# More gathered tokens in the expert layer: 112 instead of 96, one-hots weighed on ScalarE, gate matrices loaded in five parts

## The chip, the cores and the metric

One Trainium2 chip, of which the program uses one core. The metric is the device time of one execution in microseconds (us); less is better. The kernel before took 2694.28 us, the median of three runs between 2692.90 and 2695.57. The engines are TensorE (PE; PEld is its weight load), VectorE (DVE), ScalarE (ACT), GpSimd (POOL) and SyncE (SP). Each also issues DMAs, in the order of its own instructions.

## The reference

Two blocks on 512 tokens of 1024 channels, in float32. The first mixes (pooling, a state-space layer) and then runs the expert layer of this case. The second (linear attention, S5, a feed-forward network) isn't touched. Its weights and intermediate results are float32, and each has to be met closely.

```
q  = (h @ w_query)                      # 8 heads, two halves of 128
s1, s2 = scores of the halves against 128 + 128 sub-keys
v1, i1 = top_k(s1, 16);  v2, i2 = top_k(s2, 16)
top_s, pos = top_k(all 256 sums v1 + v2, 16)
idx   = i1[...] * 128 + i2[...]         # one of 16384 experts
gates = softmax(top_s)                  # 8 heads x 16 experts for each token
act   = gelu(h . expert_down[idx])      # one number per token and expert
out   = sum over (gates * act) * expert_up[idx]
```

So each token uses 128 of 16384 experts.

## The kernel before, in words

The expert layer treats its tokens in two ways. The first TG = 96 tokens are *gathered*: for each group of tokens in `GROUPS` an indirect DMA (`fetch`, L756) fetches one expert row of 1024 numbers into each of the 128 partitions, tile `row`, in 3 buffers; `dot` (L764) multiplies it with the token (VectorE, sum into `dots`). Later `weigh` (L767) takes Gelu of the dots and multiplies by the gates, and `add` (L784) fetches the row of the other matrix and adds it, weighed, to `tsum` on VectorE. A group of n tokens takes n fetches for the dots and n for the adds. The other TD = 416 tokens are *dense*: all 16384 experts are computed for them, in 128 tiles of 128 experts, and a gate matrix that is zero nearly everywhere picks out those that count.

*Down pass*, tile j: the weights are loaded (`load_w`: `raw` by SyncE's DMA, split by ScalarE into `hi`, L118, and by VectorE into the remainder `lo`, L119), then 24 matmuls (`mm3`, L126 to L128: hi x hi, hi x lo, lo x hi for 8 blocks of 128 rows) with 416 columns give `ps`; ScalarE takes Gelu (L830) and every second tile is written to HBM, `act_d`.

*Up pass*, tile j: `aj` is read back from `act_d` (L1076), `gt` holds the gates of 8 tiles (L1068, read from `g_d`, two buffers), VectorE multiplies them into `wg` (L1084), ScalarE and VectorE split this into `wh` (L131) and `wl` (L132), and 24 matmuls of 416 columns add to eight accumulators. At the end a fold (L1104) adds the gathered tokens' sums.

Beside the down pass runs a list of small jobs, `fill`, each with a cost in microseconds; after each tile `run_fill` issues as many as a due time allows. It holds the choice of experts (`select`: top 16, softmax, and `ids`, L663 to L678), the turning of the result to token order, and `scatter` (L721 to L747): for 8 dense tokens at a time VectorE compares ids with a ramp (L734, one-hots `oh`), multiplies the one half by the exponent factor of the gates (L737, `gexp`) and the other by their mantissas (L740), PE multiplies both halves into gate matrices (L745), ScalarE copies them to `gst` (L746), and every 32 tokens a DMA of POOL's queue writes a chunk of `g_d` (13 chunks). Then come the dots and the first 48 adds. Beside the up pass the list holds the other 48 adds, the tables of the S5 layer (ending with two DMAs of 2112 KB, L1015 and L1016) and some of the conditioning.

The order on each engine is not that of the source alone. A scheduler reorders by a simulated time line; `soon()` gives the chain of weights and gates priority, and `issue_after` ties an instruction behind another. The gates of tiles 8J to 8J+7 are tied behind `hi` of tile 8(J-1), four DMAs in one go.

Of the kernel before, what the change touches and what calls it, by code (L numbers as in the profile page):

```python
# [59 lines left out]
def tile_blocks(ctx, tc, I, out):  # L60
# [500 lines left out]
    with tc.tile_pool(name="peert", bufs=2, reuse_waits="tile") as pt, tc.tile_pool(name="peer", bufs=1, reuse_waits="tile") as pe:  # L561
# [63 lines left out]
        gexp = pe.tile([P, TD], BF16, name="rows_ge")  # L625
# [3 lines left out]
        def select(t):  # L629
# [31 lines left out]
            sel = [pt.tile([P, 8, 16], F32, tag=f"sel{s}", name=nm("sel"), bufs=1) for s in range(2)]  # L661

            def ids(s):  # L663
# [3 lines left out]
                else:  # L667
                    nc.vector.tensor_scalar(pi, pos, 15, None, ALU.bitwise_and)
                pf = pt.tile([P, 8, 16], F32, tag="pf", name=nm("pf"), bufs=1)
# [38 lines left out]
            def gathered():  # L708
                fid = pt.tile([P, P], F32, tag="pf", name="fid", bufs=1)
# [14 lines left out]
        def scatter(t0):  # L724

            ch, off = divmod(t0, TC)
            if off == 0:
                gst[ch] = px.tile([P, P, TC], F32, tag="g", name=nm("gst"))
# [12 lines left out]
            for c in range(n):
                ps = psum()
                for i in range(4):
                    for a in range(2):
                        nc.tensor.matmul(ps[:, i * P : i * P + P], o1[:, c, :, i], o2[a][:, c, :, i], start=a == 0, stop=a == 1)  # L745
                nc.scalar.copy(  # L746
                    gst[ch][:, :, off + 4 * c : off + 4 * c + 4].rearrange("p j t -> p t j"), ps.rearrange("p (t j) -> p t j", j=P))  # L747
            if off + SC == TC:
# [98 lines left out]
    def s5_prepare(sp):  # L847
# [183 lines left out]
        fill.append((0.1, table_out))  # L1031

    with tc.tile_pool(name="s5p", bufs=1, reuse_waits="tile") as s5p, tc.tile_pool(name="up", bufs=2, reuse_waits="tile") as pu:
# [6 lines left out]
        def beside():  # L1040
# [715 lines left out]
```

## Time and profile before

| | us |
|---|---|
| median of 3 runs | 2694.28 |
| profiled execution, its own time | 2692.56 |
| its span | 2690.7 |
| PE busy | 2597.9 (97%) |
| VectorE busy | 1874.7 (70%) |
| ScalarE busy | 1070.4 (40%) |
| GpSimd busy | 473.8 (18%) |
| down pass | 428.40 to 1102.40 |
| up pass | 1110.30 to 1729.30 |

The profile is that of one execution. Busy time says what each engine did over the whole span; the work of a pass is read in its own stretch. The chain of waits follows the end of the program back, step by step, to what released it. A releaser in brackets (`<-`) is the engine and tile that an idle engine waited for. Matmuls overlap, so a matmul's own duration is longer than the time from one start to the next. The row of a DMA issue gives its size and the time to its landing. The granted clock of TensorE was 0.985 of full speed over the span.

### The profile page before, as it was taken

The page shows a single profiled execution, that of the slowest core. Times are in us where ns is not written, and L with a number is a line of the kernel's source. Part 1 is how long each engine was busy: PE and PEld are TensorE (multiplying, and loading weights), DVE is VectorE, ACT ScalarE, POOL GpSimd, SP SyncE. Part 2 cuts the span into 40 slices and gives each one's busy share as a digit, 9 for nine tenths or more (in the row PEclk, how much of TensorE's full clock was granted, in tenths as well). Part 3 has the DMA queues.
Part 4 walks back from the last instruction along what each step waited for, and adds up shares of the span by engine and source line. Part 5 has one row for each costly group of instructions (what it writes and reads, how often), then busy time and mean ns, then how long its engine had stood idle before and what let it go on. Part 6 is the DMA issues. An engine that isn't in the chain of part 4 may idle for free.

```text
span 2690.7 us, 36274 instructions
## 1 busy us (share of the span) xinstructions
PE 2597.9 (97%) x13752; PEld 2343.2 (87%) x13752; DVE 1874.7 (70%) x3438; ACT 1070.4 (40%) x1511; POOL 473.8 (18%) x495
## 2 busy tenths in 40 slices
PE   6999999999999999899999899899999999999997
PEld 5776789999999999898999899888998888688886
DVE  5777699998898888586789457666567644552543
ACT  4574333434534445334343233445432343432221
POOL 0001000343234333111121101100053300010100
PEclk9999999999999999999999899999999999999999
DMA  6224433789888889988897978322276554233331
GB/s 259 95 84 136 145 106 121 275 287 339 299 291 307 312 302 314 318 260 297 277 302 241 290 244 271 104 79 71 83 215 190 180 176 126 73 99 94 95 101 63
DMA packets 179374, 532.93 MB, mean 198 GB/s; under 512 B 20608, under 2 KB 55648, under 8 KB 177280
## 3 DMA queue, kind: packets, MB, share of 16 engines
q1 hardware_dynamic: 85040, 280.83, 31.6%
q0 software_dynamic: 42000, 159.80, 17.7%
q10 hardware_dynamic: 52160, 89.99, 9.8%
q8 instruction: 108, 1.77, 0.3%
q14 instruction: 66, 0.54, 0.1%
HBM read 448.98 MB, written 80.41 MB: 197 GB/s over the span
## 4 chain that ended last, share of the span: by engine, by line
PE 88%; DMA 4%; DVE 3%; issue 2%; ACT 1%; ACTq 1%; POOL 0%; SPq 0%; DVEq 0%; POOLq 0%
PE ps L127 26%; PE ps L126 26%; PE ps L128 26%; PE ps L745 4%; DMA gt<-g_d 2%; DMA mats_d<-bd 1%; ACTq L1068 1%; DVE lo L119 1%; PE ps L615 1%; PE ps L1443 1%; PE ps L148 0%; ACT hi L118 0%; DMA wa<-in_wada_dram 0%; PE ps L487 0%; DMA res<-in_x_t_dram 0%
## 5 line engine op out<-in xcount | busy, mean ns | idle before, releaser
L118 ACT ACTIVATE hi<-raw 128x1024 fp32r<-128x1024 f32 (+2 forms) x459 | 481.6, 1051 | 1131.4 <-PE ps L127 811.5
L119 DVE TENSOR_TENSOR lo<-raw,hi 128x1024 fp32r<-128x1024 f32 (+2 forms) x459 | 579.7, 1265 | 373.3 <-ACT hi L118 358.7
L126 PE MATMUL ps<-h2h,hi 128*128 128x416 f32 (+1 forms) x1152 | 412.3, 359 | 4.0 <-ACT h2h L569 3.0
L127 PE MATMUL ps<-h2l,hi 128*128 128x416 f32 (+1 forms) x1152 | 413.1, 359 | 2.9 <-DVE h2l L570 2.9
L128 PE MATMUL ps<-h2h,lo 128*128 128x416 f32 (+1 forms) x1152 | 412.5, 359 | 0.0
L127 PE MATMUL ps<-wl,hi 128*128 128x416 f32 x1024 | 364.2, 356 | 17.9 <-DVE wl L132 17.9
L126 PE MATMUL ps<-wh,hi 128*128 128x416 f32 x1024 | 356.5, 355 | 10.8 <-ACT wh L131 10.8
L128 PE MATMUL ps<-wh,lo 128*128 128x416 f32 x1024 | 363.1, 356 | 1.0 <-DVE lo L119 1.0
L126 PE MATMUL ps<-Ah,hi 128*128 128x512 f32 (+2 forms) x944 | 336.4, 360 | 6.7 <-ACT Ah L1592 3.7
L127 PE MATMUL ps<-Al,hi 128*128 128x512 f32 (+2 forms) x944 | 339.7, 360 | 2.7 <-DVE Al L1130 2.7
L128 PE MATMUL ps<-Ah,lo 128*128 128x512 f32 (+2 forms) x944 | 337.0, 357 | 0.0
L126 PEld LDWEIGHTS ps<-h2h,hi 128*128 128x128 f32 x1152 | 217.9, 189 | 11.6 <-ACT h2h L569 3.8
L127 PEld LDWEIGHTS ps<-h2l,hi 128*128 128x128 f32 x1152 | 217.8, 189 | 9.9 <-DVE h2l L570 3.6
L128 PEld LDWEIGHTS ps<-h2h,lo 128*128 128x128 f32 x1152 | 218.0, 189 | 6.5 <-DVE lo L119 0.4
L756 POOL DMA_INDIRECT row<-in_eu_dram,gid x96 | 129.9, 1353 | 518.8 <-DVE tsum L784 437.1
L127 PEld LDWEIGHTS ps<-wl,hi 128*128 128x128 f32 x1024 | 194.8, 190 | 23.8 <-DVE wl L132 20.2
L126 PEld LDWEIGHTS ps<-wh,hi 128*128 128x128 f32 x1024 | 195.9, 192 | 13.9 <-ACT wh L131 11.9
L126 PEld LDWEIGHTS ps<-Ah,hi 128*128 128x128 f32 x944 | 177.8, 189 | 33.1 <-ACT Ah L1592 4.5
L127 PEld LDWEIGHTS ps<-Al,hi 128*128 128x128 f32 x944 | 178.9, 189 | 29.7 <-DVE Al L1130 2.9
L128 PEld LDWEIGHTS ps<-Ah,lo 128*128 128x128 f32 x944 | 178.6, 189 | 25.5 <-issue 1.9
L128 PEld LDWEIGHTS ps<-wh,lo 128*128 128x128 f32 x1024 | 195.5, 191 | 2.6 <-DVE lo L119 1.4
L756 POOL DMA_INDIRECT row<-in_ed_r_dram,gid x96 | 147.5, 1537 | 256.5 <-DVE dots L764 139.8
(610 smaller groups left out, 4206.6 us busy)
## 6 DMA issues: line engine op xcount, KB each, us to landing
raw<-in_ed_dram SPq DMA_DIRECT2D x128, 512.0 KB, 5.2
raw<-in_eu_dram SPq DMA_DIRECT2D x128, 512.0 KB, 4.8
raw<-in_win_dram SPq DMA_DIRECT2D x67, 512.0 KB, 3.5
raw<-in_wff_dram SPq DMA_DIRECT2D x64, 512.0 KB, 3.8
g_d<-gst POOLq DMA_DIRECT2D x13, 2048.0 KB, 9.8
aj<-act_d ACTq DMA_DIRECT2D x63, 416.0 KB, 4.5
wa<-in_wada_dram SPq DMA_DIRECT2D x46, 512.0 KB, 4.6
gt<-g_d ACTq DMA_DIRECT2D x45, 512.0 KB, 9.1
```

The costliest lines, as they stand in the source:

```text
L118: top[0] = nc.scalar.activation(hi[:, :n], raw[:, :n], AF.Copy)
L119: low[0] = nc.vector.tensor_sub(lo[:, :n], raw[:, :n], hi[:, :n].bitcast(F32))
L126: nc.tensor.matmul(ps, wh, x[0], start=first, stop=False)
L127: nc.tensor.matmul(ps, wh, x[1], start=False, stop=False)
L128: nc.tensor.matmul(ps, wl, x[0], start=False, stop=last)
L615: nc.tensor.matmul(ps[:, t * P : t * P + P], q[:, t * P : t * P + P], skt[:, m], start=True, stop=True)
L745: nc.tensor.matmul(ps[:, i * P : i * P + P], o1[:, c, :, i], o2[a][:, c, :, i], start=a == 0, stop=a == 1)
L756: nc.gpsimd.indirect_dma_start(out=raw, out_offset=None, in_=src.rearrange("a b d -> (a b) d"), in_offset=bass.IndirectOffsetOnAxis(ap=gid ...
L1068: nc.scalar.dma_start(gt[:, c:c1, a:b], g_d[c:c1, :, j // 8 * 8 + a : j // 8 * 8 + b].rearrange("c p j t -> p c j t"))
L1443: nc.tensor.matmul(ps[:, 16 * i : 16 * i + 16], wk[:, i, j * P : j * P + P], wk[:, i, c0 : c0 + 16], start=j == 0, stop=j == 1)
```

## The change

- `GROUPS` gets a third group of 16 tokens: 112 gathered, 400 dense. All dense matmuls have 400 columns.
- The chunks of `g_d` hold 24 tokens, and the last 16 have a tensor of their own, `ge_d`: 16 chunks and one small.
- `scatter` multiplies the one-hots by the exponents on ScalarE, one instruction of 128x128 for each token (L745 of the changed kernel).
- In `ids` the positions are 16-bit numbers, and the sum over 16 places is made by halving.
- A dot is computed two fetches after its own (`dots_of`), `row` has 4 buffers. 96 dots and 56 adds are listed in the down pass; 16 dots, the weighing of groups two and three and 56 adds in the up pass. The due times and some buffers change with it.
- The gates of the next 8 tiles come in five DMAs (L1099 and L1101), each tied behind `hi` of another of the five tiles 8(J-1) to 8(J-1)+4. `wg` is made by two multiplies, of 384 and 16 columns (L1137 and L1138).
- The two 2112 KB DMAs of the S5 tables are issued in eight parts.

```diff
-    TC = 32
-    GROUPS = ((0, 64, 2), (64, 32, 4))
+    TC = 24
+    GROUPS = ((0, 64, 2), (64, 32, 4), (96, 16, 8))
     TG = sum(n for _, n, _ in GROUPS)
     TD = T - TG
-    NCH = TD // TC
+    NCH, TE = divmod(TD, TC)
     g_d = dp.tile([NCH, P, P, TC], F32, name="g_d")
+    ge_d = dp.tile([P, P, TE], F32, name="ge_d")
...
-                pf = pt.tile([P, 8, 16], F32, tag="pf", name=nm("pf"), bufs=1)
+                pf = pt.tile([P, 8, 16], F16, tag="pf", name=nm("pf"), bufs=1)
...
-                nc.vector.tensor_reduce(sel[s], eq, AX.X, ALU.add)
+                for n in (8, 4, 2):
+                    nc.vector.tensor_tensor(eq[:, :, :, :n], eq[:, :, :, :n], eq[:, :, :, n : 2 * n], ALU.add)
+                nc.vector.tensor_tensor(sel[s], eq[:, :, :, 0], eq[:, :, :, 1], ALU.add)
...
-            nc.vector.tensor_tensor(
-                o1, eq[:, :, 0], bc(gexp[:, t0 : t0 + SC].rearrange("p (c t) -> p c t", t=4).unsqueeze(2), [P, n, P, 4]), ALU.mult)
+            for t in range(SC):
+                nc.scalar.mul(o1[:, t // 4, :, t % 4], eq[:, t // 4, 0, :, t % 4], gexp[:, t0 + t : t0 + t + 1])
...
-            raw = gx.tile([P, D], F32, tag="row", name=nm("row"), bufs=3)
+            raw = gx.tile([P, D], F32, tag="row", name=nm("row"), bufs=4)
...
+        def dots_of(lag):
+            while len(asked) > lag:
+                g, i, raw = asked.pop(0)
...
         def dot(g, i):
-            raw = fetch(I["ed_r"], g, i)
...
+            asked.append((g, i, fetch(I["ed_r"], g, i)))
+            dots_of(2)
...
-        NOW, LAST = 48, 16
+        NOW, LAST = 56, 24
...
-        dots_, adds_ = [dot_of(p) for p in picks[n0:]], adds[: NOW - LAST]
+        dots_, adds_, left = [dot_of(p) for p in picks[n0 : n0 + 32]], adds[: NOW - LAST], [dot_of(p) for p in picks[n0 + 32 :]]
...
-        per = sum(c for c, _ in fill) / (P - 6)
+        per = sum(c for c, _ in fill) / (P - 10)
...
-            run_fill(min((j + 1) * per - done[0], 4.8))
+            run_fill(min((j + 1) * per - done[0], 5.0))
...
-        def table_out():
-            nc.gpsimd.dma_start(mats_d[:, :, MW - 2 * NC5 : MW - NC5], et["r"])
-            nc.gpsimd.dma_start(mats_d[:, :, MW - NC5 :], et["i"])
+        def table_out(a):
+            nc.gpsimd.dma_start(mats_d[:, a : a + 8, MW - 2 * NC5 : MW - NC5], et["r"][:, a : a + 8])
+            nc.gpsimd.dma_start(mats_d[:, a : a + 8, MW - NC5 :], et["i"][:, a : a + 8])
...
+        def gate_piece(to, b, i, j0, j1):
+            of = slice(8 * b + j0, 8 * b + j1)
+            if i < NPC - 1:
+                c = slice(4 * i, min(4 * i + 4, NCH))
+                nc.scalar.dma_start(to[0][:, c, j0:j1], g_d[c, :, of].rearrange("c p j t -> p c j t"))
+            else:
+                nc.scalar.dma_start(to[1][:, j0:j1], ge_d[:, of])
...
-                with tc.issue_after(tops[max(j - 8, 0)].ins) if j else ExitStack():
-                    for c in range(0, NCH, 4):
-                        c1 = min(c + 4, NCH)
-                        nc.scalar.dma_start(gt[:, c:c1, a:b], g_d[c:c1, :, j // 8 * 8 + a : j // 8 * 8 + b].rearrange("c p j t -> p c j t"))
...
+            with tc.issue_after(top[0].ins):
+                if j == 2:
+                    for i in range(NPC):
+                        gate_piece(cur, 0, i, 4, 8)
+                if j % 8 == 0 and j < P - 8:
+                    nxt = gate_tile()
+                if j % 8 < 5 and j < P - 8:
+                    for i in range(j % 8, NPC, 5):
+                        gate_piece(nxt, j // 8 + 1, i, 0, 8)
...
-                nc.vector.tensor_tensor(
-                    wg.rearrange("p (c t) -> p c t", t=TC), aj[j % 2].rearrange("p (c t) -> p c t", t=TC), gt[:, :, j % 8], ALU.mult)
+                nc.vector.tensor_tensor(v(wg), v(aj[j % 2]), gt[:, :, j % 8], ALU.mult)
+                nc.vector.tensor_tensor(wg[:, NCH * TC :], aj[j % 2][:, NCH * TC :], ge[:, j % 8], ALU.mult)
```

The change moves instructions; two places are shown. The first is the seam between the passes, on ScalarE. Before, with the gates of tiles 0 to 3 (`gt_1483`) and of tiles 8 to 15 (`gt_1540`) issued around the last but one Gelu (`at_`), and `hi` of tile 1 behind them (`hi_1493`):

```order
725 L1068 DMA gt_1483_10124<-g_d_2335 128x4x128 x3
726 L830 ACTIVATE at__1479_10067<-ps355_10036 128x416
727 L1068 DMA gt_1483_10124<-g_d_2335 128x128
728 L1068 DMA gt_1540_10506<-g_d_2335 128x4x256 x3
729 L1068 DMA gt_1540_10506<-g_d_2335 128x256
730 L118 ACTIVATE hi_1493_10170<-raw_1492_10169 128x1024
731 L830 ACTIVATE at__1479_10067<-ps356_10069 128x416
732 L118 ACTIVATE hi_1500_10212<-raw_1499_10211 128x1024
733 L832 DMA act_d_2336<-at__1479_10067 128x832
734 L1076 DMA aj_1498_10209<-act_d_2336 128x832
735 L131 ACTIVATE wh_1490_10140<-wg_1489_10139 128x416
```

Afterwards, from `wh` of tiles 0 and 1 (`wh_1493`, `wh_1499`) to `wh` of tile 2 (`wh_1506`); `gt_1485` are the gates of tiles 0 to 7, of which these are 4 to 7, and `gt_1491` those of tiles 8 to 15:

```order
789 L118 ACTIVATE hi_1503_10591<-raw_1502_10590 128x1024
790 L1099 DMA gt_1485_10501<-g_d_2335 128x4x96 x4
791 L1101 DMA gt_1485_10501<-ge_d_2336 128x64
792 L1099 DMA gt_1491_10517<-g_d_2335 128x4x192
793 L118 ACTIVATE hi_1509_10634<-raw_1508_10633 128x1024
794 L1099 DMA gt_1491_10517<-g_d_2335 128x4x192
795 L865 DMA s5in_10671<-in_s5_dram 128x2144
796 L205 DMA cs_1514_10685<-in_c_dram 128x1024
797 L118 ACTIVATE hi_1517_10691<-raw_1516_10690 128x1024
798 L1101 DMA gt_1491_10517<-ge_d_2336 128x128
799 L1117 DMA aj_1515_10688<-act_d_2337 128x800
800 L131 ACTIVATE wh_1506_10603<-wg_1505_10602 128x400
```

What moved: the gate transfers that stood in front of `hi` of tile 1 and of `wh` of tile 0 are now spread, a piece behind the `hi` of each of tiles 0 to 4 (the first two stand ahead of these rows), with the rest of tiles 4 to 7 behind the `hi` of tile 2; and `wh` of tile 2 comes after the `hi` of tile 4.

The second place is the change from one group of gates to the next, on VectorE, where `wg` of tile 16 is made. Before, behind `lo` of tile 10:

```order
1570 L119 TENSOR_TENSOR lo_1557_10625<-raw_1555_10623,hi_1556_10624 128x1024
1571 L883 TENSOR_TENSOR s5_pr3_10289<-s5_t0_10555,s5_t1_10556 128x32
1572 L132 TENSOR_TENSOR wl_1560_10631<-wg_1558_10629,wh_1559_10630 128x416
1573 L1084 TENSOR_TENSOR wg_1600_10907<-aj_1596_10899,gt_1595_10894 128x416
1574 L1084 TENSOR_TENSOR wg_1607_10946<-aj_1596_10899,gt_1595_10894 128x416
```

Afterwards, behind `lo` of tile 12:

```order
1616 L119 TENSOR_TENSOR lo_1580_11110<-raw_1578_11108,hi_1579_11109 128x1024
1617 L897 TENSOR_TENSOR s5_t0_10952<-s5_e2r_11204 128x32
1618 L898 TENSOR_TENSOR s5_t1_10953<-s5_e2i_11205 128x32
1619 L1137 TENSOR_TENSOR wg_1611_11320<-aj_1606_11310,gt_1550_10913 128x384
1620 L1137 TENSOR_TENSOR wg_1619_11362<-aj_1606_11310,gt_1550_10913 128x384
1621 L897 TENSOR_TENSOR w16_1622_11394<-s5_fr_11187,s5in_10671 128x512
1622 L132 TENSOR_TENSOR wl_1583_11117<-wg_1581_11115,wh_1582_11116 128x400
1623 L898 TENSOR_TENSOR w16_1623_11395<-s5_fi_11188,s5in_10671 128x512
1624 L899 TENSOR_TENSOR s5_er_11202<-s5_t0_10952,s5_t1_10953 128x32
1625 L1138 TENSOR_TENSOR wg_1611_11320<-aj_1606_11310,gt_1550_10913 128x16
1626 L1138 TENSOR_TENSOR wg_1619_11362<-aj_1606_11310,gt_1550_10913 128x16
```

And on ScalarE the pieces that these wait for, behind `hi` of tiles 10, 11 and 12 (the rows start behind the `hi` of tile 10):

```order
827 L1099 DMA gt_1550_10913<-g_d_2335 128x4x192
828 L1117 DMA aj_1624_11402<-act_d_2337 128x800
829 L118 ACTIVATE hi_1570_11065<-raw_1569_11064 128x1024
830 L1099 DMA gt_1550_10913<-g_d_2335 128x4x192
831 L131 ACTIVATE wh_1573_11072<-wg_1572_11071 128x400
832 L118 ACTIVATE hi_1579_11109<-raw_1578_11108 128x1024
833 L1101 DMA gt_1550_10913<-ge_d_2336 128x128
```

What moved: `wg` of tile 16 went from two tiles behind the issue of its gates to right behind `lo` of tile 12, the tile whose `hi` stands just before the last piece; the products of that piece (L1138) are placed six instructions later than the others.

## Rows read from the trace of the kernel before

**Rows 1.** The chain that ended last, share of the span by line.

```profile
PE 88%; DMA 4%; DVE 3%; issue 2%; ACT 1%; ACTq 1%; POOL 0%; SPq 0%; DVEq 0%; POOLq 0%
PE ps L127 26%; PE ps L126 26%; PE ps L128 26%; PE ps L745 4%; DMA gt<-g_d 2%; DMA mats_d<-bd 1%; ACTq L1068 1%; DVE lo L119 1%; PE ps L615 1%; PE ps L1443 1%; PE ps L148 0%; ACT hi L118 0%; DMA wa<-in_wada_dram 0%; PE ps L487 0%; DMA res<-in_x_t_dram 0%
```

**Rows 2.** Stretches: length, busy time of PE, PEld, DVE, ACT, POOL, clock, DMA share, GB/s.

```profile
428.40:1102.40 674.00, 672.91 (x3895) 651.57 (x3894) 595.96 (x956) 305.76 (x381) 231.30 (x173) 1.00 0.84 294
1110.30:1729.30 619.00, 596.80 (x3104) 586.48 (x3104) 443.91 (x752) 219.83 (x303) 88.93 (x70) 0.98 0.80 262
600.00:700.00 100.00, 100.00 (x610) 95.41 (x609) 88.22 (x121) 50.41 (x59) 35.97 (x28) 1.00 0.90 323
494.00:1080.00 586.00, 584.91 (x3422) 564.09 (x3421) 520.74 (x777) 272.62 (x335) 215.73 (x152) 1.00 0.87 307
1500.00:1520.00 20.00, 14.68 (x63) 14.27 (x64) 10.74 (x16) 6.00 (x8) 0.00 (x0) 0.72 0.81 225
```

**Rows 3.** Groups of instructions by line and form: count, busy us, mean ns, idle before.

```profile
L126 PE MATMUL ps<-h2h,hi 128*128 128x416 f32 x1024 | 361.0, 353 | 1.1 <-ACT hi L118 1.1
```

**Rows 4.** PE in order of time: start us, us, instruction; and the fold's group.

```profile
1080.31 0.35 PE L127 MATMUL ps<-h2l,hi 128*128 128x416 f32 x1
...
1102.34 0.34 PE L128 MATMUL ps<-h2h,lo 128*128 128x416 f32 x1
...
2399.63 0.39 PE L127 MATMUL ps<-Al,hi 128*128 128x512 f32 x1
...
2402.35 0.39 PE L127 MATMUL ps<-Al,hi 128*128 128x512 f32 x1
...
2661.86 0.28 PE L126 MATMUL ps<-Bh,hi 128*128 128x256 f32 x1
...
2664.57 0.28 PE L128 MATMUL ps<-Bh,lo 128*128 128x256 f32 x1
...
609.14 1.81 PE L745 MATMUL ps<-o,o 128*128 128x128 f16 x14
...
L1104 PE MATMUL ps<-fold,tsum 128*128 128x32 f32 x16 | 2.9, 262 | 0.0
```

**Rows 5.** PE's waits in the up pass: us in total, times, longest.

```profile
PE ps L127 <- DVE wl L132: 17.9, 7, 10.6
PE ps L126 <- ACT wh L131: 10.8, 3, 7.6
PE ps L128 <- DVE lo L119: 1.0, 1, 1.0
```

**Rows 6.** Seam and one late gate, in order of time, idle time before in brackets.

```profile
1098.25 8.52 ACTq L1068 DMA_DIRECT2D gt<-g_d  x5
...
1106.81 1.06 ACT L118 ACTIVATE hi<-raw 128x1024 fp32r<-128x1024 f32 x1 [8.05 <-issue]
...
1502.54 0.59 DVE L1084 TENSOR_TENSOR wg<-aj,gt 128x416 f32<-128x416 f32 x1 [18.72 <-DMA gt<-g_d]
...
1505.32 0.71 PE L127 MATMUL ps<-wl,hi 128*128 128x416 f32 x1 [10.64 <-DVE wl L132]
```

**Rows 7.** Landing times of the gate tile's DMAs.

```profile
DMA to landing us min/median/max: 4.1/9.2/24.7
```

**Rows 8.** DMA issues, 1110 to 1710: count, KB each, median us to landing.

```profile
aj<-act_d ACTq DMA_DIRECT2D x62, 416.0 KB, 4.5
...
gt<-g_d ACTq DMA_DIRECT2D x14, 128.0 KB, 11.7
```

**Rows 9.** Groups on VectorE and ScalarE that price the moved work.

```profile
L737 DVE TENSOR_TENSOR o<-oh,rows_ge 128x1024 bf16<-128x1024 f16 x52 | 35.7, 687 | 0.1
...
L430 ACT ACTIVATE sg<-ps,acs 128x128 f32<-128x128 f32 x64 | 18.5, 392 | 6.0 <-PE ps L427 6.0
...
L688 ACT COPY ge<-ps 128x128 f32<-128x128 f32 x4 | 1.0, 259 | 2.1 <-PE ps L686 2.1
...
L784 DVE SCALAR_TENSOR_TENSOR tsum<-row,ggate,tsum 128x1024 f32<-128x1024 f32 x48 | 61.4, 1278 | 0.0
...
L1084 DVE TENSOR_TENSOR wg<-aj,gt 128x416 f32<-128x416 f32 x128 | 72.2, 588 | 58.0 <-DMA gt<-g_d 46.2 <-DMA aj<-act_d 9.6 <-issue 1.1
```

More of the change, by code (lines that the diff above doesn't have):

```diff
@@ L572, in tokens_of @@
         def tokens_of():
-            tok = gx.tile([P, D], F32, tag="row", name="tok", bufs=3)
+            tok = gx.tile([P, D], F32, tag="row", name="tok", bufs=4)
             for i in range(2):
@@ L624, in tile_blocks @@
         rows, gate2 = (pe.tile([P, TD // 4, 2, 4], F16, name="rows_" + n) for n in ("i", "g"))
-        gexp = pe.tile([P, TD], BF16, name="rows_ge")
+        gexp = pe.tile([P, TD], F32, name="rows_ge")
+        iota16 = pe.tile([P, 16], F16, name="iota16")
+        nc.vector.tensor_copy(iota16, iota[:, :16])
         iota4 = pe.tile([P, P, 4], F16, name="iota4")
@@ L660, in select @@
             fill.append((1.0, softmax))
-            sel = [pt.tile([P, 8, 16], F32, tag=f"sel{s}", name=nm("sel"), bufs=1) for s in range(2)]
+            sel = [pt.tile([P, 8, 16], F32, tag=("top", "sel1")[s], name=nm("sel"), bufs=1) for s in range(2)]
             def ids(s):
@@ L708, in gathered @@
             def gathered():
-                fid = pt.tile([P, P], F32, tag="pf", name="fid", bufs=1)
+                fid = pt.tile([P, P], F32, tag="pos", name="fid", bufs=1)
                 s0, s1 = (a.rearrange("p h k -> p (h k)") for a in sel)
@@ L727, in scatter @@
             if off == 0:
-                gst[ch] = px.tile([P, P, TC], F32, tag="g", name=nm("gst"))
+                gst[ch] = px.tile([P, P * TC], F32, tag="g", name=nm("gst"))
+            tc_ = TC if ch < NCH else TE
+            to = gst[ch][:, : P * tc_].rearrange("p (j t) -> p j t", t=tc_)
             n = SC // 4
@@ L786, in add @@
         def add(g, i, lag):
+            dots_of(2)
             pending.append((g, i, fetch(I["eu"], g, i)))
@@ L810, in tile_blocks @@
                     down.append(l.pop(0))
-        down += [(0.1, lambda g=g: weigh(g)) for g in range(1, len(GROUPS))]
         share = sum(c for c, _ in down) / sum(c for c, _ in todo)
@@ L1030, in s5_prepare @@
             a += n
-        fill.append((0.1, table_out))
+        for a in range(0, NPAIR, 8):
+            fill.append((2.0, lambda a=a: table_out(a)))
     with tc.tile_pool(name="s5p", bufs=1, reuse_waits="tile") as s5p, tc.tile_pool(name="up", bufs=2, reuse_waits="tile") as pu:
@@ L1047, in beside, with weights @@
             fill.clear()
-            gathers = adds[NOW:] + [(0.1, lambda: sums_of(0))]
+            def weights():
+                with tc.issue_after(top[0].ins):
+                    for g in range(1, len(GROUPS)):
+                        weigh(g)
+            n0 = GROUPS[0][1]
+            gathers, ones = [], adds[NOW : n0 - 3]
+            for i, d in enumerate(left):
+                gathers.append(d)
+                if i % 2 == 1 and ones:
+                    gathers.append(ones.pop(0))
+            gathers += ones + [(0.1, lambda: dots_of(0))] + adds[n0 - 3 : n0 - 1] + [(0.1, weights)] + adds[n0 - 1 :] + [(0.1, lambda: sums_of(0))]
             share = sum(c for c, _ in gathers) / sum(c for c, _ in rest)
@@ L1079, in tile_blocks @@
             tops.append(top[0])
+            with tc.issue_after(top[0].ins):
+                if j == 2:
+                    for i in range(NPC):
+                        gate_piece(cur, 0, i, 4, 8)
[4 more added lines that the diff above has]
+                        gate_piece(nxt, j // 8 + 1, i, 0, 8)
+            if j % 8 == 7 and j < P - 8:
+                cur = nxt
             wg = tp.tile([P, TD], F32, tag="t", name=nm("wg"))
```

26 lines of the change are left out of this document (17 added, 9 removed).

## The prediction

> **What bounds the kernel now.** Read first the chain that ended last: TensorE holds 88% of it, and 78 of the 88 points are the three products of `mm3`, 26% each; VectorE holds 3%, ScalarE 1%, transfers 4%, of which the gate tiles `gt` are 2% [rows 1]. Then cut the span into stages. In the down pass (428.40 to 1102.40) PE is busy 672.91 of 674.00 us at granted clock 1.00, VectorE 595.96, ScalarE 305.76: whoever is second hides behind PE. In the up pass PE is busy 596.80 of 619.00 at clock 0.98 [rows 2]. So there are two prices: work taken from PE counts in full in both passes, and in the up pass there are waits to win back besides.
>
> **What a column costs.** A matmul's own duration is no price, since neighbours overlap (353 ns each in the group [rows 3]); read the pitch from start to start. 416 columns: 1080.31 to 1102.34 in 118 steps, 0.1867 us. 512 columns: 2399.63 to 2402.35 in 12 steps, 0.2267. 256: 2661.86 to 2664.57 in 23 steps, 0.1178 [rows 4]. The slope is (0.2267-0.1867)/96 = 0.417 ns a column, or (0.1867-0.1178)/160 = 0.431. The 256-column row also says that loading weights sets no floor near 400 columns. 112 gathered tokens leave 400 dense ones: 16 columns fewer, 6.67 to 6.89 ns a matmul. The matmuls are 24 (eight row blocks by three) times 128 expert tiles in each pass, 6144 (one of the six groups: 1024 [rows 3]): -41.0 to -42.3 us, taken **-41.5**.
>
> **Scatter.** 400 dense tokens make 100 fours instead of 104, each eight matmuls: 32 fewer. Fourteen in a row took 1.81 us [rows 4], with about 0.30 of tail (1.81-0.30)/13 = 0.116 each: **-3.7**. At the end of the up pass a fold adds the gathered tokens' sums to the output, 16 steps for each group [rows 4]. The third group adds 16, between 0 and 16 x 0.116 = 1.9, since nothing covers PE there nearly all of it: **+1.4**. PE's work falls by 43.8.
>
> **The weighing on ScalarE.** 52 VectorE multiplies of 687 ns, 35.7 us [rows 9], become 50 x 8 = 400 ScalarE ones of 128x128. The nearest rows bound one: 259 ns for a plain copy of that shape, 392 for an activation with a scale per partition [rows 9], so 104 to 157 us; by the nearer row, the second, 157. ScalarE goes from 306 to at most 463 us of some 650, VectorE falls. Hidden by PE, unless a scatter comes late: the eight stand between the compare and PE's scatter, in one buffer, and behind them on ScalarE's queue wait `hi` of the next weights and the Gelu. Bounds: 0, and half a microsecond at each of 50 scatters, 25 us. With the order leaving PE between half a tile and three tiles (a tile is 24 x 0.1867 = 4.5 us and its scatter) after them I take **+3**. Ids in 16 bits and the halving sums are VectorE work under the same cover: 0, from -1 to +2.
>
> **Gathered tokens.** 16 more dots and 8 more adds in the up pass at 1278 ns [rows 9] make 30.7 us, and the second, 16-wide product of gates costs 128 times something between 0 and a whole one's 588 ns [rows 9], 0 to 75, by its width near the low end: 15. VectorE goes from 443.91 to about 490 of some 580. Hidden on average: 0, and if that cover fails, the third rival. The weighing (Gelu, product) is moved up too; its ScalarE step waits for the last dot, and `hi` and `wh` are behind it. It happens once: 0 to 5, taken 0. On POOL's queue, from which rows are fetched, two table transfers become eight; a fourth row buffer and dots that lag by two loosen VectorE's waits for rows. All of this is off PE's path: 0, between -2 and +2.
>
> **Waits won back.** 3072 matmuls of 0.1867 and 32 fold steps of 0.116 make 577 of the up pass's 619.00: some 41.6 are lost, 22.1 in PE's waits there and 19.5 in a lower clock and small gaps. With the seam ahead (1102.40 to 1110.30, 7.9) it is 49.5. PE's waits are 29.7 in all: 17.9 for `wl`, 10.8 for `wh`, 1.0 for `lo` [rows 5]. Two are large. At the seam five gate DMAs hold ScalarE's queue 8.52 us, and `hi` starts 8.05 late [rows 6]; PE waits 7.6 [rows 5]. At 1502.54 VectorE's `wg` has waited 18.72 for `gt`, and PE 10.64 at 1505.32 [rows 6], so PE bears some 8.1 of such a wait; from 1500 to 1520 the granted clock is 0.72, partly at its lower level of 1.2 GHz, the idle engine ahead of it [rows 2].
> After the change the next group's pieces go out one a tile, in the seam two before `wh` of tile 0. Yet in the order `wh` of tile 2 now stands behind `hi` of tile 4, and behind it the other pieces: 2.5 us at each of tiles 2 and 4, so 5 for 7.9. The 10.64 goes; the 11.5 of small waits (22.1-10.6) I leave. Waits then fall from 29.7 to 16.5, and I let clock and gaps fall in that ratio, 19.5 to 10.8. Left: 5+11.5+10.8 = 27.3 of 49.5, **-22.2**. Bounds: -49.5 and 0.
> What is late next: `wg` of tile 8J was one or two tiles behind its gates' issue; now it stands right behind `lo` of the tile after whose `hi` the last piece goes out. That piece is the smallest, and only the 16-wide products need it. A `gt` landing took 4.1 to 24.7 us, median 9.2 [rows 7]: past 8.1 and some 3 of other work PE would feel it.
> Size bears little on landing here: 416 KB of `aj` alone took 4.5 us, the 128 KB of `gt` issued fourth in its row 11.7 [rows 8]; place in the queue does. The Trainium skill ("DMA: Bandwidth & Descriptors", Bandwidth) states the reverse emphasis: batch transfers to at least 1 MiB, since each has about 2 us of fixed cost; as an estimate from that page a fifth transfer in each of 15 groups is 30 us of queue, which on the path would make 2660. The trace disagrees as far as these landings go.
>
> **Sum.** -41.5 -3.7 +1.4 +3 -22.2 = -63.0, against the profiled execution's 2692.56 (span 2690.7; the median of the runs is 2694.28, 1.7 more): **2630 us**. With its own bounds (returned waits from 42 to 12, scatter from 0 to 10) the likeliest case is 2607 to 2647.
>
> **Rivals.**
> *Transfers pace the down pass.* The stretch 494 to 1080 moved 307 GB/s at share 0.87, 180 MB; the best 100 us 323 at 0.90 [rows 2]. Afterwards the fill is to end four tiles sooner and each tile is shorter: 586 x 118/122, less 20.5 (its part of the 24.4 that columns and scatter save in this pass), is 546 us, for about 179.4 MB (8 more gathers, 4 tiles fewer): 328 GB/s. At 323 that takes 555, +9; at 307 584, +38. For it: no stretch has kept 328. Against: rate over share says 353 to 359 at a full share, and PE did not wait at 0.90. 2639 to 2668, about 2655. The Trainium skill (the same page, "Where 436 GB/s comes from") gives some 358 GB/s as a core's share of HBM; it agrees with 323/0.90, and by it this rival stays away.
> *No wait is left*: -49.5 for -22.2, and 0 for the scatter: 2600. Against it the order at tiles 2 and 4.
> *Slower: gates pace VectorE.* In each of 15 groups `wg` waits for its pieces, with `lo` and `wl` behind it on VectorE and PE behind these. Above 8.1 us of wait each microsecond is PE's. The gain is used up at 63/15 = 4.2 a group, a wait of 12.3, which the median landing of 9.2 does not give but the long ones do. At 14 us it is 6 a group: 2630+90 = 2720. Against: four of five pieces have a tile or more of lead, and alone in the queue.
> *It doesn't do what it says:* the 16 columns save nothing (a floor at the 416-column pitch): 2630+41.5 = 2672. Against: the 256-column row.
>
> **Chances.** Forecast 0.60; transfers 0.20; no wait left 0.09; columns without effect 0.03; slower 0.05; the rest, within 0.2% (about 5 us, what a measurement of this kernel can tell from none), 0.03. All but the last two are faster: 0.92. The range takes the forecast's and most of the first two: 2602 to 2668.
>
> **What would show it.** Matmul starts 0.180 us apart in both passes; down pass 650 us with PE at 99%; 400 multiplies of 0.26 to 0.39 on ScalarE; at the seam PE waits of 2 to 3 us twice in place of one of 7.6; no wait of VectorE for `gt` over 10 us, and the up pass near 580. Wrong would be: a pitch of 0.187, PE waiting for `hi` or `lo` of late weights in the down pass, or 15 regular waits in the up pass.

## The result, and the profile after

The changed kernel took 2651.68 us, the median of four runs (2650.59 to 2654.36), beside 2693.59 for the kernel before: ratio 0.9852, 95% interval 0.9829 to 0.9874. Two later sets of runs gave 2653.92 and 2654.82. The forecast was 2630 with a range of 2602 to 2668: faster as foretold, but by 42 us and not by 63. The profiled execution took 2650.59, 41.97 less than the one before.

The stages first, in the columns of [rows 2]; the down pass runs to 1084.90, the up pass behind it:

```profile
421.00:1084.90 663.90, 655.87 (x3895) 633.93 (x3894) 576.50 (x968) 450.71 (x782) 258.60 (x205) 1.00 0.85 304
1084.90:1687.90 603.00, 569.39 (x3115) 564.99 (x3114) 468.49 (x916) 222.02 (x306) 134.91 (x97) 0.98 0.84 289
```

From its first dense matmul the down pass fell from 679.8 us (422.77 to 1102.53) to 663.8 (421.13 to 1084.88), 16.0 less. From there to the fold's last group the up pass with its seam fell from 626.2 to 603.0, 23.2 less. The start is 1.6 earlier and the rest of the program 1.1 shorter: 41.9, the difference of the spans (2690.7 and 2648.8).

The pitch of the matmuls, in the down pass (start us, us, instruction; it answers to the first two of [rows 4]):

```profile
1074.80 0.34 PE L127 MATMUL ps<-h2l,hi 128*128 128x400 f32 x1
...
1084.70 0.34 PE L128 MATMUL ps<-h2h,lo 128*128 128x400 f32 x1
```

55 steps in 9.90 us are 0.180 each, the 0.180 forecast. 0.0067 times 6144 matmuls is 41 us: as much as the whole kernel gained. So the rest of the change comes to nothing in sum, and the 22 us of waits to be won back don't show in the time. PE's waits in the up pass, with the seam (in total, times, longest), answer to [rows 5]:

```profile
PE ps L126 <- ACT wh L131: 17.4, 2, 11.0
PE ps L127 <- DVE wl L132: 13.9, 6, 8.5
PE ps L128 <- DVE lo L119: 2.1, 1, 2.1
```

33.4 us, where it was 29.7 and 16.5 was forecast. The two waits for `wh` both stand at the seam. ScalarE there, in order of time (ACTq is its queue of transfers), and PE's two waits; they answer to [rows 6]:

```profile
1085.99 0.44 ACTq L1117 DMA_DIRECT2D aj<-act_d  x1
1086.54 1.06 ACT L118 ACTIVATE hi<-raw 128x1024 fp32r<-128x1024 f32 x1 [0.95 <-DVE wl L132]
1086.55 9.18 ACTq L1099 DMA_DIRECT2D gt<-g_d  x4
1095.77 2.64 ACTq L1101 DMA_DIRECT2D gt<-ge_d  x1
1098.45 0.45 ACTq L1099 DMA_DIRECT2D gt<-g_d  x1
1099.00 1.06 ACT L118 ACTIVATE hi<-raw 128x1024 fp32r<-128x1024 f32 x1 [11.40 <-DMA gt<-g_d]
...
1104.18 1.09 ACT L131 ACTIVATE wh<-wg 128x400 fp32r<-128x400 f32 x2 [2.51 <-DVE wg L1138]
```

```profile
1104.77 3.00 PE L126 MATMUL ps<-wh,hi 128*128 128x400 f32 x8 [11.02 <-ACT wh L131]
...
1121.38 3.04 PE L126 MATMUL ps<-wh,hi 128*128 128x400 f32 x8 [6.38 <-ACT wh L131]
```

Five gate transfers in a row, those of tiles 4 to 7, hold ScalarE 11.8 us: a transfer that takes 0.45 to issue by itself takes 2.3 in such a row. `hi` of tile 3 comes 11.4 late, and `wh` of tile 2 behind it. A row of five stood in the seam of before too (8.52 us): the last piece of tiles 4 to 7 (not 0 to 3, as written above: those had gone out between 1060 and 1090) and four of tiles 8 to 15. The change sends those of tiles 8 to 15 one a tile, and has the five of tiles 4 to 7 in a row.

The late gate is there too. The eight parts of the S5 tables leave POOL in one go, since all wait for the last of VectorE's work on them:

```profile
1488.99 3.63 POOL L1031 DMA_DIRECT2D mats_d<-s5e  x4 [10.05 <-DVE s5e L899]
1492.60 3.52 POOL L1032 DMA_DIRECT2D mats_d<-s5e  x4
```

and 25 us behind the issue of the last large gate piece (1497.98) VectorE gets it, and PE waits:

```profile
1523.15 0.56 DVE L1137 TENSOR_TENSOR wg<-aj,gt 128x384 f32<-128x384 f32 x1 [12.56 <-DMA gt<-g_d]
```

```profile
1524.25 0.70 PE L127 MATMUL ps<-wl,hi 128*128 128x400 f32 x1 [8.52 <-DVE wl L132]
```

In the down pass PE waited 1.1 us before. Now it is 8.0:

```profile
PE ps L128 <- DVE lo L119: 4.6, 3, 2.8
PE ps L126 <- ACT hi L118: 2.7, 3, 1.2
PE ps L752 <- ACT o L745: 0.7, 2, 0.4
```

### The profile page after: what moved, and what is told of

The parts are those of the page before. It is cut to its first block, busy times and chain, and to the rows that moved or that the text cites. A ratio compares the mean times of both kernels' runs of the same rounds, so it can differ in the third digit from the quotient of the medians.

```text
span 2648.8 us, 36985 instructions
## 1 busy us (share of the span) xinstructions
PE 2546.2 (96%) x13736; PEld 2299.6 (87%) x13736; DVE 1873.0 (71%) x3583; ACT 1212.0 (46%) x1909; POOL 550.7 (21%) x561
## 4 chain that ended last, share of the span: by engine, by line
PE 82%; DMA 6%; DVE 5%; ACT 4%; issue 2%; POOL 0%; ACTq 0%; SPq 0%; DVEq 0%; POOLq 0%
PE ps L126 24%; PE ps L127 24%; PE ps L128 24%; DMA gt<-g_d 3%; PE ps L752 3%; DMA raw<-in_eu_dram 1%; ACT gst L753 1%; DVE lo L119 1%; ACT o L745 1%; ACT hi L118 1%; DMA mats_d<-bd 1%; PE ps L616 1%; PE ps L1496 1%; PE ps L148 1%; PE ps L487 0%
## 5 line engine op out<-in xcount | busy, mean ns | idle before, releaser
L126 PE MATMUL ps<-h2h,hi 128*128 128x400 f32 (+1 forms) x1152 | 405.2, 353 | 5.7 <-ACT h2h L570 3.0
L127 PE MATMUL ps<-h2l,hi 128*128 128x400 f32 (+1 forms) x1152 | 405.9, 352 | 2.9 <-DVE h2l L571 2.9
L128 PE MATMUL ps<-h2h,lo 128*128 128x400 f32 (+1 forms) x1152 | 403.8, 352 | 4.6 <-DVE lo L119 4.6
L127 PE MATMUL ps<-wl,hi 128*128 128x400 f32 x1024 | 353.7, 345 | 13.9 <-DVE wl L132 13.9
L126 PE MATMUL ps<-wh,hi 128*128 128x400 f32 x1024 | 343.1, 348 | 17.5 <-ACT wh L131 17.4
L128 PE MATMUL ps<-wh,lo 128*128 128x400 f32 x1024 | 346.7, 344 | 2.1 <-DVE lo L119 2.1
L763 POOL DMA_INDIRECT row<-in_eu_dram,gid x112 | 174.9, 1561 | 405.3 <-DVE tsum L800 290.5
L763 POOL DMA_INDIRECT row<-in_ed_r_dram,gid x112 | 162.2, 1448 | 252.8 <-DVE dots L775 142.7
L126 PEld LDWEIGHTS ps<-wh,hi 128*128 128x128 f32 x1024 | 194.3, 190 | 18.8 <-ACT wh L131 18.2
```

The costliest lines, as they stand in the source:

```text
L126: nc.tensor.matmul(ps, wh, x[0], start=first, stop=False)
L127: nc.tensor.matmul(ps, wh, x[1], start=False, stop=False)
L128: nc.tensor.matmul(ps, wl, x[0], start=False, stop=last)
L763: nc.gpsimd.indirect_dma_start(out=raw, out_offset=None, in_=src.rearrange("a b d -> (a b) d"), in_offset=bass.IndirectOffsetOnAxis(ap=gid ...
```

## Experiments

All are edits of the changed kernel, timed beside runs of the kernel before on the same chip. Times are medians, with the ratio to the kernel before and its 95% interval.

**The changed kernel again**, with the next three.

> The changed kernel once more, beside the next three on the same chip: 2650 to 2655 us. Both theories say the same; it is the level that the others are held against.

2653.92 us, 0.9872 (0.9846 to 0.9897). Its waits at the seam are 12.4 and 6.4, the one at the tables 10.5.

**The first gates whole.**

```diff
-                        gate_piece(cur, 0, i, 0, 4)
+                        gate_piece(cur, 0, i, 0, 8)
...
-                if j == 2:
-                    for i in range(NPC):
-                        gate_piece(cur, 0, i, 4, 8)
```

> The gates of tiles 0 to 7 are loaded whole, in five transfers, during the down pass, so that the five transfers of tiles 4 to 7 no longer stand on ScalarE's queue behind hi of tile 2. Theory A (the queue: these five held ScalarE 11.8 us, and PE waited 11.0 for wh of tile 2): that wait falls under 2 us, the one of 6.4 at tile 4 stays at 3 to 6, since it hangs on VectorE's order, and the time falls by 8 to 13 us against the changed kernel. Rival B (the transfers as a whole pace the seam: the bytes are the same): the wait comes back at another tile there, and the time falls by less than 3 us.

2654.88 us, 0.9876 (0.9850 to 0.9902): nothing gained, as rival B said. The waits at the seam fell from 18.8 to 10.8. The first of the two that are left (5.85) stands behind `hi` of tile 4, 5.8 us late: on ScalarE's queue the issue of the S5 inputs and of the conditioning's rows takes 3.35 and 2.45 us ahead of it. The larger gate transfers now go out in the down pass from 1041 on, and there something else is late: ScalarE waits for a write of `act_d`, and PE for `lo`:

```profile
1065.16 0.51 ACT L846 ACTIVATE at__1467_10310<-ps 128x400 f32<-128x400 f32 x1 [5.40 <-DMA act_d<-at__1453_10178]
```

```profile
1067.62 0.70 PE L128 MATMUL ps<-h2h,lo 128*128 128x400 f32 x1 [5.25 <-DVE lo L119]
...
1106.08 3.04 PE L126 MATMUL ps<-wh,hi 128*128 128x400 f32 x8 [5.85 <-ACT wh L131]
```

**The tables spread** (`gots` lists the weights' transfers by tile).

```diff
+            for i, n in enumerate("ri"):
+                with tc.issue_after(gots[92 + a // 2 + 2 * i].ins):
+                    nc.sync.dma_start(mats_d[:, a : a + 8, MW - (2 - i) * NC5 : MW - (1 - i) * NC5], et[n][:, a : a + 8])
```

> The eight transfers of the S5 tables (4.2 MB) go out on SyncE's queue, one behind the weights of every second tile from 92 on, instead of eight at once on GpSimd's queue. Theory A (the eight at once made the last gate piece land 25 us late, VectorE waited 12.6 and PE 8.5): no wait of VectorE for gt over 8 us in that place, PE's 8.5 gone, the time falls by 8 to 12 us. Rival B (load as a whole): the same bytes in the same pass, so PE's wait turns up as waits for raw, and the time falls by less than 3 us.

2647.15 us, 0.9840 (0.9813 to 0.9868), 6.8 below the changed kernel beside it; the intervals overlap, so the time alone doesn't settle it. The trace does as far as the mechanism goes: PE's longest wait for `wl` in the up pass is 2.7, and no wait of 8 stands there.

```profile
PE ps L127 <- DVE wl L132: 7.4, 5, 2.7
```

But part of the price came back, as rival B said: SyncE's queue also brings the weights, `hi` of one tile waits 10.0 us for them, and PE waits 2.4 and 2.7 behind it. So 5.1 us stand in the place of 8.5.

```profile
1547.95 1.06 ACT L118 ACTIVATE hi<-raw 128x1024 fp32r<-128x1024 f32 x1 [9.98 <-DMA raw<-in_eu_dram]
```

```profile
1549.49 0.45 PE L126 MATMUL ps<-wh,hi 128*128 128x400 f32 x1 [2.38 <-ACT wh L131]
...
1552.67 0.70 PE L127 MATMUL ps<-wl,hi 128*128 128x400 f32 x1 [2.73 <-DVE wl L132]
```

**Both.**

> Both edits. Theory A: they touch different places, so the gains add: 16 to 24 us below the changed kernel, near 2630. Rival B: less than 5 us.

2653.00 us, 0.9869 (0.9845 to 0.9893). The gains did not add: a wait of 3.6 near the end of the down pass and 7.9 and 4.7 at the seam stand against what the tables gave. Theory A, that five transfers on ScalarE's queue are the whole matter at the seam, can't stand in this form.

**Without the columns.**

```diff
-    GROUPS = ((0, 64, 2), (64, 32, 4), (96, 16, 8))
+    GROUPS = ((0, 64, 2), (64, 32, 4))
```

> The changed kernel with the third group of gathered tokens taken out again: 96 gathered, 416 dense, everything else as changed. My theory, that the columns are nearly the whole gain: the pitch is 0.187 again, 41.5 for the columns, 3.7 for the scatter, 1.4 less fold, so 44 us above the changed kernel, 2694 to 2700, level with the kernel before. Rival (the gate pieces, the moved weighing and the rest are worth something of their own): 2675 to 2688.

2693.07 us (12 runs), 1.0012 (0.9997 to 1.0028): level with the kernel before, 39 us above the changed one. The columns and the scatter are the gain, and all other edits together come to nothing at 416 columns. But that nothing is a sum of two parts that cancel. In the columns of [rows 2], the down and the up pass (with its seam) of this run:

```profile
420.04:1116.73 696.69, 684.83 (x3926) 660.02 (x3924) 581.60 (x971) 463.43 (x802) 244.53 (x188) 0.99 0.81 293
1116.73:1727.89 611.16, 589.39 (x3101) 581.53 (x3101) 439.60 (x868) 222.27 (x305) 82.62 (x66) 0.98 0.80 261
```

and between the same bounds of the kernel before:

```profile
422.77:1102.53 679.76, 678.67 (x3925) 657.17 (x3923) 601.24 (x984) 308.56 (x384) 231.39 (x173) 1.00 0.83 292
1102.53:1728.73 626.20, 596.47 (x3102) 586.11 (x3102) 445.74 (x755) 222.31 (x306) 88.42 (x70) 0.97 0.80 264
```

So with as many matmuls the down pass is 16.9 us longer (PE waits 11.8 in it for 1.1: 5.6 for `o`, weighed by ScalarE, 5.5 for `lo`, 0.7 for `o` of VectorE), and the up pass 15.0 shorter (waits of 21.8 for 29.7, and 7 us less of busy time, at a granted clock of 0.98 for 0.97). The late gate is there as well:

```profile
PE ps L127 <- DVE wl L132: 14.1, 2, 12.1
PE ps L126 <- ACT wh L131: 7.7, 2, 6.3
```

The waits for `wh` are smaller than with 112 tokens (7.7 and 17.4): the same row of gate transfers, six here, took 6.4 us.

**Gates at once.**

```diff
-                if j % 8 < 5 and j < P - 8:
-                    for i in range(j % 8, NPC, 5):
+                if j % 8 == 0 and j < P - 8:
+                    for i in range(NPC):
```

> The five pieces of the next group's gates all go out behind hi of tile 8(J-1), as the four did before, instead of one a tile. Theory A (what is late is late for other reasons, the table transfers and the seam): VectorE's waits for gt stay within 10 us of the changed kernel's 34.8, PE's 10.6 or 8.5 stays, the time is within 4 us. Rival: the spreading keeps ScalarE's queue free, and without it hi comes 5 to 10 us late in 15 groups: slower by 10 us or more.

2667.57 us, 0.9905 (0.9884 to 0.9926): by the ratios 6 to 14 us slower than the three timings of the changed kernel. The interval is apart from that of the first only, but four of the six runs are slower than every run of the changed kernel. So sending the five apart is worth something, as the rival said, if perhaps less than its 10. In [rows 6] and [rows 7] the four of before came late too, but here, beside the table transfers, the row of five holds ScalarE 21.6 us:

```profile
1494.04 11.81 ACTq L1099 DMA_DIRECT2D gt<-g_d  x2
1505.89 10.11 ACTq L1101 DMA_DIRECT2D gt<-ge_d  x1
1516.11 1.06 ACT L118 ACTIVATE hi<-raw 128x1024 fp32r<-128x1024 f32 x1 [21.64 <-issue]
```

```profile
1517.64 0.70 PE L126 MATMUL ps<-wh,hi 128*128 128x400 f32 x1 [11.84 <-ACT wh L131]
```

The small fifth one took 1.7 us in the median, 10.1 at most, where it takes 0.34 when it goes out alone. VectorE's waits for `gt` are halved meanwhile (16.5 us against 34.8): the price is paid on ScalarE's queue.

How long a row holds ScalarE depends on what else is moving. Of the 14 rows behind the seam, the nine with the transfers' share at 0.74 to 0.92 took 2.8 to 4.8 us and once 6.9. Of the five with 0.98 to 1.04 four took 5.9 to 12.2, and the one beside the tables 22.9 from its first issue to its last. One row of the first kind, and the stretches of one of the second kind and of this one (columns of [rows 2]):

```profile
1272.52 0.94 ACTq L1099 DMA_DIRECT2D gt<-g_d  x2
1273.48 0.52 ACT L131 ACTIVATE wh<-wg 128x400 fp32r<-128x400 f32 x1
1273.48 1.09 ACTq L1099 DMA_DIRECT2D gt<-g_d  x2
1274.88 0.43 ACTq L1101 DMA_DIRECT2D gt<-ge_d  x1
```

```profile
1234.22:1246.37 12.15, 12.15 (x69) 12.13 (x67) 6.59 (x13) 2.60 (x4) 4.79 (x4) 1.00 1.03 376
1272.52:1275.31 2.79, 2.79 (x17) 2.78 (x16) 2.79 (x9) 1.48 (x2) 0.00 (x0) 1.00 0.77 248
```

**The weighing on VectorE.**

```diff
-        gexp = pe.tile([P, TD], F32, name="rows_ge")
+        gexp = pe.tile([P, TD], BF16, name="rows_ge")
...
-            for t in range(SC):
-                nc.scalar.mul(o1[:, t // 4, :, t % 4], eq[:, t // 4, 0, :, t % 4], gexp[:, t0 + t : t0 + t + 1])
+            nc.vector.tensor_tensor(
+                o1, eq[:, :, 0], bc(gexp[:, t0 : t0 + SC].rearrange("p (c t) -> p c t", t=4).unsqueeze(2), [P, n, P, 4]), ALU.mult)
```

> The one-hots are weighed on VectorE again, one multiply of 687 ns for 8 tokens. Theory A (the 8.0 us of PE's waits in the down pass are mostly VectorE's pile-up when experts are chosen, where lo is late): those waits stay or grow, by 0 to 4 us, and ScalarE's 137 us in these multiplies cost PE some 1.7. Rival: ScalarE's load is the cause of all eight, and the time falls by 5 to 8.

`gexp` is in 16 bits again, as in the kernel before. 2658.47 us, 0.9866 (0.9843 to 0.9889). By its median 3.7 to 6.8 above the changed kernel, by the ratios no different. The rival falls (nothing became faster). In the trace PE's waits at the choice of experts, where `lo` is late, are 3.4 in place of 4.6, and 6.8 for scatters that come last (1073 to 1085) join them. Elsewhere the order moved too: the seam has one wait of 19.1, and PE waits 5.4 for `hi` at 1639. At 112 tokens ScalarE's weighing is no cost to speak of, and no large gain.

**The side work later.**

```diff
-            if j == 3:
+            if j == 11:
                 beside()
-                per = sum(c for c, _ in fill) / (P - 10)
+                per = sum(c for c, _ in fill) / (P - 18)
```

> The work beside the up pass (the loads of the S5 inputs and of the conditioning, 1.6 MB on ScalarE's queue, their table load, and the small VectorE work) begins at tile 11 instead of tile 3. Theory A (the order on VectorE and ScalarE at the seam): PE's 6.4 at tile 4 falls under 2, the 11 to 12 at tile 2 stays above 8 since the five gate transfers still stand there; 4 to 8 us faster. Rival B (the transfers at the seam are saturated, 362 GB/s at share 1.01): with 1.6 MB less in 20 us, 4.4 us of transfers, both waits shrink, and the 11 goes under 7.

2666.58 us, 0.9904 (0.9882 to 0.9926): by the ratios 6 to 14 slower, against both. At the seam it went half as A said: 11.8 stays, 6.4 becomes 4.6. The five transfers held ScalarE as long:

```profile
1087.99 9.94 ACTq L1099 DMA_DIRECT2D gt<-g_d  x4
1097.98 2.65 ACTq L1101 DMA_DIRECT2D gt<-ge_d  x1
```

That doesn't settle A against B, since the S5 inputs stood behind the row: from 1085 to 1125 only 276 GB/s moved on average (317 with the changed kernel), but not while the row was issued. There the load is that of the changed kernel. This run's stretch, and that of the changed kernel:

```profile
1088.00:1100.00 12.00, 7.18 (x40) 6.85 (x38) 2.46 (x3) 1.04 (x1) 0.95 (x1) 0.94 1.05 385
```

```profile
1086.50:1098.50 12.00, 7.25 (x40) 6.92 (x39) 2.37 (x3) 1.06 (x1) 0.95 (x1) 0.95 1.05 384
```

No run had this row of five under a lower load at the seam; the rows of *gates at once* are the nearest. The loss came later: the same side work in fewer tiles, with waits of 2.0 and 3.3 for `wl` at 1249 and 1276 and of 13.6 at the tables, 1574.

**The first gates early, one a tile** (`downs` lists `hi` of the down pass's tiles).

```diff
+            downs.append(top[0])
...
+                    for i in range(NPC):
+                        with tc.issue_after(downs[122 + i].ins):
+                            gate_piece(cur, 0, i, 4, 8)
...
-                if j == 2:
-                    for i in range(NPC):
-                        gate_piece(cur, 0, i, 4, 8)
```

> The five transfers of the gates of tiles 4 to 7 go out in the down pass, one behind each of hi of its tiles 122 to 126, instead of in one go behind hi of tile 2 of the up pass; sizes and bytes are as in the changed kernel. Theory A (what PE waits for at the seam is ScalarE, held 12 us by five transfers in a row on its own queue): the wait of 11 to 12 at tile 2 falls under 3, that of 6.4 at tile 4 to 3 to 6, no new wait over 2 in the down pass, and the time falls by 8 to 14 us against the changed kernel, to 2639 to 2645. Rival B (all transfers together are at their limit there, share 0.95 to 1.03 from 1025 to 1105, as when the gates were loaded whole): the same bytes earlier make others late, a new wait of 4 us or more appears in the down pass, and the time stays within 4 us.

2650.55 us, 0.9856 (0.9837 to 0.9876); its five runs spread from 2644 to 2657, and 4 us can't be told from none. No new wait over 2 us stands near the end of the down pass, as A has it. At the seam PE waits 8.1 and 2.5 in place of 11 to 12 and 6.4: more than A allowed. A piece of tiles 8 to 15, twice as large as those of the row and sent by itself, takes 0.38 us to issue there, at a share of 1.05 and 392 GB/s (1088 to 1094); the S5 inputs behind the fourth, a single transfer of 1072 KB, take 5.8:

```profile
1093.25 0.38 ACTq L1101 DMA_DIRECT2D gt<-g_d  x1
1093.66 5.82 ACTq L867 DMA_DIRECT2D s5in<-in_s_dram  x1
```

**Early, and the tables spread.**

> The same, with the table transfers spread on SyncE's queue as well. Theory A: 5 to 9 us below gates_early, 2632 to 2640. Rival B: 2645 to 2650, no better than the spread tables alone.

2638.18 us (2636.30 to 2639.51), 0.9804 (0.9791 to 0.9818). Its interval is apart from those of the changed kernel (the nearest 0.9829 to 0.9874): this version beats both kernels, the changed one by 14 to 17 us. By the medians the two edits gain at least what they gain apart (1 to 4 and 5 to 8, neither of them clear of noise). The longest wait in the up pass is now 5.9, at tile 2. Behind it stands a transfer, that of `aj` for tiles 2 and 3, for which VectorE waits; it lands 12.1 us after its issue, where the median was 4.5 [rows 8]:

```profile
1099.26 0.56 DVE L1141 TENSOR_TENSOR wg<-aj,gt 128x384 f32<-128x384 f32 x1 [5.70 <-DMA aj<-act_d]
```

in a stretch in which the transfers are at their most (columns of [rows 2]):

```profile
1085.00:1105.00 20.00, 14.08 (x69) 13.46 (x68) 12.83 (x22) 5.81 (x7) 5.44 (x4) 0.83 1.04 391
```

**The S5 inputs on SyncE's queue**, with a third timing of the changed kernel.

```diff
-        nc.scalar.dma_start(inp, I["s5"])
+        nc.sync.dma_start(inp, I["s5"])
...
-            with tc.issue_after(top[0].ins):
+            with tc.issue_after(top[0].ins), tc.issue_after(got[0].ins):
                 s5_prepare(s5p)
```

> The changed kernel a third time, the level beside which the next one stands: 2648 to 2656 us.

> As early_and_spread, and the S5 inputs (1072 KB) are loaded on SyncE's queue behind the weights of tile 3, not on ScalarE's. In gates_early their issue held ScalarE 5.8 us ahead of wh of tile 2. Theory A (ScalarE's own queue): the wait at tile 2 falls from 5.9 to under 3, that at tile 4 grows by up to 2.5, since a second activation table is now loaded ahead of wh of tile 4; 1 to 5 us faster than early_and_spread, 2633 to 2638. Rival B (the bytes, whoever issues them): the weights behind these inputs come late in the place of ScalarE, the wait at tiles 2 to 4 stays at 8 or more in sum, the time at 2636 to 2641.

The changed kernel took 2654.82 us, 0.9882 (0.9861 to 0.9904), this one 2641.95, 0.9825 (0.9804 to 0.9846): not better than early_and_spread, though its time can't be told from it. Rival B's waits came: 10.0 and 1.2 at the seam, 11.1 in sum. ScalarE isn't held by these inputs any more, and `wg` waits for `aj` all the same:

```profile
1102.45 0.56 DVE L1141 TENSOR_TENSOR wg<-aj,gt 128x384 f32<-128x384 f32 x1 [5.58 <-DMA aj<-act_d]
```

```profile
1103.71 1.70 PE L126 MATMUL ps<-wh,hi 128*128 128x400 f32 x4 [9.99 <-ACT wh L131]
```

## Why the prediction was right in the main and 21 us short

**Columns, right.** The pitch came out as the slope of [rows 4] gave it, and taking the third group out cost 39 us, where the sum had 41.5+3.7-1.4 = 43.8. The range is another matter. With its own bounds the forecast's case reached from 2607 to 2647, and 2651.68 lies outside; it lies in the range only because that was widened for the rival of the transfers, whose 2655 is nearer and whose mechanism didn't come. That is luck.

**The down pass, mis-sized.** +3 was taken; PE's waits there grew by 6.9 (1.1 to 8.0), and the pass fell by 16.0 where 20.7+3.7-3 = 21.4 was forecast. The reason given was ScalarE's weighing, whose waits (`hi` and `o`) are 3.4. The larger part, 4.6, are waits for `lo` while VectorE is busy without a gap (40.00 of 40 us from 700 to 740) with the choice of experts and dots. That VectorE, with less to do in the whole pass (576 us for 596), has less room in that place (37.50 of 40 us before) was not looked at. It doesn't come from the columns: with 96 tokens and the other edits the pass is 16.9 longer than before (tokens_96). Part of it may be the new order of the dots; no run took them apart.

**Waits won back, the step that failed.** "2.5 us at each of tiles 2 and 4, so 5 for 7.9" became 17.4; "the 10.64 goes" became 8.5; only the small waits did better (7.5 for 11.5). Left were 33.4 for 16.5, 16.9 of the 18.4 us by which the up pass missed. Clock and gaps fell to 10.9 (569.4 us busy, less 3072 x 0.180 and 48 x 0.116), where 10.8 was forecast in the ratio of the waits; as the waits grew, that is luck too.
At the seam the two places were right and the prices were not. The price was on hand: five gate transfers on ScalarE's queue took 8.52 us [rows 6]. The prediction followed the order to the place where they now stand ("behind it the other pieces") and priced `wh` of tile 2 by the distance in tiles alone. The runs show what that left out. The row holds ScalarE 12 us at a share of 1.05. At the same load pieces twice as large, sent one a tile, take 0.38 each (gates_early), and five such in a row take mostly 3 to 5 us where the share is below 0.93 (gates_at_once): it takes the row and the load together. With the row gone other things are late in the same stretch: ScalarE behind the issue of the S5 inputs (gates_whole, gates_early), and `aj`, late by 5.7 at 391 GB/s (early_and_spread) and by 5.6 with the inputs on another queue (inputs_on_sync). That `aj` is late because of the load is argued from its landing of 12 us; no run lightened the load in that place.
At the tables the prediction put the late gate down to its place in its own queue, and so let it go with the five parts. The cause was the 4.2 MB of tables beside it: sent out over 15 tiles on SyncE's queue, they leave PE no wait for the gate, though 5.1 us for late weights (tables_spread), and cutting them in eight without spreading them changed little (8.5 to 10.5 for 10.64).

**The rivals.** Transfers did not pace the down pass as a whole: 304 GB/s on average, and 350 at share 0.97 from 1000 to 1085 without a wait of PE for weights. At the seam, where no rival had put them, they have a part. The Trainium skill ("DMA: Bandwidth & Descriptors", "Where 436 GB/s comes from"), cited for a share of 358 GB/s, is no ceiling here: 391 over 20 us, with one core running. Slower did not come: VectorE waited 34.8 us for `gt` in six places, not in 15 groups; and where the pieces go out at once the price falls on ScalarE, not on VectorE. The rule of the Trainium skill to batch to 1 MiB (same page, Bandwidth) would speak for fewer, larger transfers. Twice as large and half as many at the seam, they gained nothing (gates_whole); that the same ones are better apart than in a row is another comparison. The 30 us of queue estimated for a fifth transfer in 15 groups didn't come: sent apart it took 0.34 us in the median and 4.2 once.

**Seen and not priced.** That the edits other than the columns come to nothing at 96 tokens was not foretold: 19 us were expected of them (22.2 less 3). There the up pass did win 15.0 of the 22.2; the down pass lost 16.9 where 3 were taken.

## What to carry to other kernels

Price what leaves the engine that is busy 97% of the time by the pitch of its instructions; that part of the sum held. Do not credit a stall as gone because its instruction moved: name what it waited for, and carry the price of the whole group of instructions to the place where the new order puts it. Transfers issued in a row on the queue of an engine that also computes hold that engine, longest while the DMA engines are full (12 us for five at a share of 1.05); one for each step of its own work cost it 0.4 us each here. And compare loads over the stretch in which the issue waits: an average over a longer one can hide that two runs had the same load there.

## What the runs showed of the hardware

An issue of gates on ScalarE's queue takes 0.33 to 0.60 us when sent apart (69 of the changed kernel's 70 behind the seam; once 4.2), also while the transfers' share is over 1. Five in a row took 11.8 us at a share of 1.05 and 2.8 to 4.8 mostly below 0.93; beside 4.2 MB of other writes two took 11.8 and one 10.1. A single transfer of 1072 KB took 5.8. In the seam ScalarE computed nothing for 11.4 us meanwhile.
Comparing ids in 16 bits did not make the compare faster (2278 ns before, 2282 now; no run shows why); the halving sums did a little: 2277 ns for one `tensor_reduce` before, 686+436+434+415 now. The compare now, by line, engine and shape, with the mean ns:

```profile
L675 DVE TENSOR_TENSOR eq<-pf,iota 128x2048 f16<-128x2048 f16 x8 | 18.3, 2282 | 0.0
```

ScalarE's 400 multiplies are busy 137.3 us, 343 ns each in a row, inside the bounds of 259 and 392, while one by itself is 567 from start to end:

```profile
L745 ACT ACTIVATE o<-oh,rows_ge 128x128 bf16<-128x128 f16 x400 | 137.3, 567 | 7.3 <-DVE oh L741 2.9 <-DVE rows_ge L703 2.5 <-ACT at__1317_9216 L846 0.4
```
